# Accumulating DMAs in place of VectorE additions for the weight sums of a seven-product matrix multiplication

## The chip, the cores and the metric

The kernel runs on one core of a Trainium2 chip. A core has a matrix engine (TensorE, "PE" in the profile; its weight loads are "PEld"), a vector engine (VectorE, "DVE"), an activation engine (ScalarE, "ACT"), a general engine (GpSimd, "POOL") and a queue engine that mostly starts transfers (SyncE, "SP"). Each works through its own instructions in order and waits on semaphores for the others. Transfers (DMAs) are started from the queue of SP, ACT or POOL and carried out by 16 DMA engines. Data is worked on in SBUF (128 partitions); matrix products land in PSUM, which has eight banks here.

The metric is the device time of one execution in microseconds (us), as the median of several runs.

## The reference

Two sequences, 512 and 256 tokens of 1,024 features, go through two layers with shared weights. Each layer adds a SwiGLU feed-forward block, a token mixer and a second feed-forward block, all behind RMSNorms:

```
def swiglu_ffn(x, w1, w2):
    gate, up = jnp.split(x @ w1, 2, axis=-1)
    return (jax.nn.silu(gate) * up) @ w2

for li in range(DEPTH):                                   # DEPTH = 2
    x = x + 0.5 * swiglu_ffn(rmsnorm(x, norm_g[li, 0]), ffn_w1[li, 0], ffn_w2[li, 0])
    h = rmsnorm(x, norm_g[li, 1])
    x = x + mixer(h)           # a gated linear recurrence in layer 0, windowed attention in layer 1
    x = x + 0.5 * swiglu_ffn(rmsnorm(x, norm_g[li, 2]), ffn_w1[li, 1], ffn_w2[li, 1])
return rmsnorm(x, final_norm_g)
```

All is float32. `w1` is 1,024 x 5,632 (gate and up side by side), `w2` is 2,816 x 1,024. There are four feed-forward blocks, called f0 to f3 below.

## The kernel before

**Tiling of a feed-forward block.** The 768 tokens of both sequences are handled together, features on the partitions. The 2,816 hidden features are 22 blocks of 128, in groups of 2, 4, 4, 4, 4 and 4. For each group the kernel computes the hidden blocks ("up phase") and then multiplies them with their rows of `w2` and adds the result to x ("down phase"). Every operand is split into a high part (rounded to the matrix engine's float32r format) and a low part (the rest), and every product is three matmuls: high·high, high·low, low·high (`mm3`, lines 234 to 236).

**The seven-product pair.** The first group (2 blocks) uses plain products (`up_plain`). In the other five groups each hidden block is one pair of a gate tile and an up tile, each 1,024 x 128, multiplied with Strassen's scheme in Winograd's form (`up_pair`, from line 504): the two weight tiles are cut into halves a11, a12 (gate, first and last 512 rows) and a21, a22 (up), and the tokens into two halves of 384. Seven products of half size replace eight. They run on PE in the order p1, p6, p2, p7, p5, p4, p3, each as 12 matmuls of 384 columns (line 494). A pair has four PSUM banks, a, b, c and d, and between the products VectorE and ScalarE read them: for example `w = c - v` (line 516) reads bank c after p7 and must have read it before p4 accumulates into the same bank. The products need four sums of weight blocks: s3 = a11 + a21, a21 + a22, a11 + (a21 + a22), and a12 + that.

**Staging of weights.** `load_next` starts the loads of raw weights from SyncE into four buffers of 512 KB (`wr`), so two pairs at a time. `pair_steps` gives seven steps, one for each product. A step forms its sum on VectorE (lines 177, 178, 179 and 183) and calls `split` (lines 165 to 170): a ScalarE cast makes the high part (line 167), a VectorE subtraction the low part (line 168; on GpSimd for p5 alone). The result goes into one of eight buffers (`w`, `WBUFS`). When PE has finished a product, `done` frees its buffer and `ahead` stages the next step; so in the up phase the cast of a product waits until PE has finished the product eight places before it. Weights of the first group and of `w2` are split without sums (lines 152 and 153) and take two buffers each.

**Start of a block.** The token side needs sums too (t1 to t4 for each of four blocks, `sum_steps`, lines 411 to 414), formed on GpSimd while PE runs the first group's plain products; each is then split by ScalarE and VectorE (lines 239 and 240). After them, in ScalarE's order, come the activations of the plain products (line 485) and the split of their hidden block (line 239), which the first down phase waits for.

**Order.** A scheduler places the instructions of each engine when the program is built, from dependences and its own cost model; within an engine the order is then fixed. Buffers of one tag are used in turn; a new tile waits until the readers of the old one are done.

The functions that the change touches, with the line numbers that the profile of this kernel uses:

Of the kernel before, what the change touches and what calls it, by code (L numbers as in the profile page):

```python
# [9 lines left out]
F32 = mybir.dt.float32  # L10
# [3 lines left out]
ALU = mybir.AluOpType  # L14
AX = mybir.AxisListType

P = 128
# [4 lines left out]
TA, TB = 512, 256  # L22
# [20 lines left out]
class Trunk:  # L43
# [22 lines left out]
        return t[:, :n]  # L66

    def tmp(self, n, dt=F32):
        tag, bufs, size = ("tA", 9, TA) if n > TB else ("tB", 4, TB)
        t = self.tp.tile([P, size], dt, tag=tag, name=self.name(tag), bufs=bufs)  # L70
        return t[:, :n]

# [61 lines left out]
    def load_next(self):  # L134
        key, srcs, shape, eng = self.queue.pop(0)
        raws = []
        for src in srcs:
            t = self.wp.tile([P, 1024], F32, tag="wr", name=self.name("wr"), bufs=RAWBUFS)
            raw = t[:, : shape[0] * shape[1]].rearrange("p (a b) -> p a b", a=shape[0])
            self.last_load = self.nc.sync.dma_start(raw, src.rearrange("(k p) c -> p k c", p=P))  # L140
            raws.append(raw)
        steps = self.plain_steps(key, raws[0], shape, eng) if len(raws) == 1 else self.pair_steps(key, *raws)
        self.loaded.append((len(raws), steps))

    def wtile(self):
        return self.wp.tile([P, 1024], F32R, tag="w", name=self.name("w"), bufs=WBUFS)
# [8 lines left out]

        return [(2, go)]

    def pair_steps(self, key, one, two):
        nc = self.nc
        flat = lambda t, h: t[:, h * 4 : h * 4 + 4, :].rearrange("p a b -> p (a b)")  # L160
        a11, a12, a21, a22 = flat(one, 0), flat(one, 1), flat(two, 0), flat(two, 1)
        box = {}

        def split(name, src, eng):
            w = self.wtile()
            hi, lo = w[:, :512], w[:, 512:]
            nc.scalar.copy(hi, src)  # L167
            eng.tensor_sub(lo, src, hi.bitcast(F32))  # L168
            view = lambda t: t.rearrange("p (a b) -> p a b", a=4)
            self.staged[(*key, name)] = (view(hi), view(lo), 1)  # L170

        def p1():
            split("p1", a11, nc.vector)

        def p6():
            box["s3"] = self.tmp(512)
            nc.vector.tensor_add(box["s3"], a11, a21)  # L177
            nc.vector.tensor_add(a21, a21, a22)
            nc.vector.tensor_add(a11, a11, a21)
            split("p6", a11, nc.vector)  # L180

        def p3():
            nc.vector.tensor_add(a12, a12, a11)
            split("p3", a12, nc.vector)

        return [
            (1, p1),
            (1, p6),
            (1, lambda: split("p2", a12, nc.vector)),
            (1, lambda: split("p7", box["s3"], nc.vector)),  # L190
            (1, lambda: split("p5", a21, nc.gpsimd)),
            (1, lambda: split("p4", a22, nc.vector)),
            (1, p3),
        ]

    def stage_next(self):
# [223 lines left out]
    h = [None, None]  # L420
# [939 lines left out]
```

## Time and profile before

| | |
|---|---|
| median of 3 runs | 3043.2 us (3041.46 to 3043.63) |
| the profiled execution: time, span | 3045.14 us, 3043.3 us |
| mean granted TensorE clock | 0.978 |
| PE busy / PEld busy | 2935.9 us (96%) / 2722.8 us (89%) |
| DVE busy | 2013.2 us (66%), 3510 instructions |
| ACT busy | 1175.8 us (39%) |
| POOL busy | 570.2 us (19%), 414 instructions |
| moved by DMAs | 207.61 MB, 68 GB/s over the span |

Busy shares are averages over stages with different limits. A row of the groups of instructions names line, engine, operation, output and inputs with shape, and the count; after the first bar stand busy time in us and the mean of one in ns; after the second bar the idle time of the engine just before them and what ended it. In the timeline the columns are start, duration, engine, line, operation, operands, count, and in brackets the idle time before with its releaser. Names carry no buffer number: `wr` is a raw weight buffer, `w` a staged one, `ps` a PSUM bank, `big` an activation tile.

### The profile page before, as it was taken

To read this page: it belongs to the slowest core of one execution; us is meant where nothing else is said; L and a number is where in the kernel's file an instruction comes from. 1 tells how busy PE (TensorE), PEld (TensorE's weight loads), DVE (VectorE), ACT (ScalarE), POOL (GpSimd) and SP (SyncE) were. 2 spreads that over 40 slices of the span, in tenths; PEclk is the share of its full clock that TensorE was granted. 3 is DMA by queue.
4 is the path that set the end of the run, shared out by engine and by line. 5 is a ranking of instruction groups with operands and counts; after the bars stand their busy time and mean duration, and the time that the engine had idled before them with its cause. 6 is when DMAs were issued, how large, how long until landed. Compare 5 with 4: busy or idle time off the path is not lost. (4 is left out here: it accounts for less than half of the span.)

```text
span 3043.3 us, 42529 instructions
## 1 busy us (share of the span) xinstructions
PE 2935.9 (96%) x16805; PEld 2722.8 (89%) x16805; DVE 2013.2 (66%) x3510; ACT 1175.8 (39%) x2233; POOL 570.2 (19%) x414
## 2 busy tenths in 40 slices
PE   6999999999999999999999899999999998999998
PEld 6999999788898888999998899999887777999998
DVE  5766666467577667666666766666659867666665
ACT  5333334433333333333324333333457743333323
POOL 3000000344444123000002300000202433000001
PEclk8999999999999999999999899999999998999999
DMA  3212223321111231222123122212411111222122
GB/s 119 73 56 70 70 70 92 97 62 36 40 51 29 82 99 42 63 77 83 57 66 100 30 76 78 72 54 70 131 63 56 42 42 42 63 76 83 56 67 94
DMA packets 292041, 207.61 MB, mean 68 GB/s; under 512 B 7208, under 2 KB 275968, under 8 KB 291840
## 3 DMA queue, kind: packets, MB, share of 16 engines
q1 hardware_dynamic: 281920, 191.45, 21.1%
q10 hardware_dynamic: 9920, 13.43, 1.3%
q8 instruction: 132, 2.16, 0.3%
q14 instruction: 69, 0.57, 0.1%
HBM read 195.42 MB, written 9.44 MB: 67 GB/s over the span
## 5 line engine op out<-in xcount | busy, mean ns | idle before, releaser
L494 PE MATMUL ps<-big,w 128*128 128x384 f32 x6720 | 1171.1, 334 | 0.0
L494 PEld LDWEIGHTS ps<-big,w 128*128 128x128 f32 x6720 | 1163.4, 188 | 3.7 <-DVE tA L518 3.7
L234 PE MATMUL ps<-big,w 128*128 128x256 f32 (+2 forms) x2304 | 793.8, 347 | 30.9 <-ACT big L239 30.9
L235 PE MATMUL ps<-big,w 128*128 128x256 f32 (+2 forms) x2304 | 789.4, 343 | 6.8 <-DVE big L240 4.1
L236 PE MATMUL ps<-big,w 128*128 128x256 f32 (+2 forms) x2304 | 784.6, 341 | 0.0
L167 ACT CAST w<-wr 128x512 fp32r<-128x512 f32 x480 | 290.1, 621 | 834.1 <-issue 330.4
L234 PEld LDWEIGHTS ps<-big,w 128*128 128x128 f32 x2304 | 444.7, 193 | 78.9 <-ACT big L239 35.3
L235 PEld LDWEIGHTS ps<-big,w 128*128 128x128 f32 x2304 | 445.8, 193 | 51.5 <-DVE big L240 6.5
L236 PEld LDWEIGHTS ps<-big,w 128*128 128x128 f32 x2304 | 444.7, 193 | 42.0
L168 POOL TENSOR_TENSOR w<-wr,w 128x512 fp32r<-128x512 f32 x80 | 102.9, 1286 | 1656.2 <-ACT w L167 1656.2
L542 DVE SCALAR_TENSOR_TENSOR x<-ps,x 128x512 f32<-128x512 f32 (+1 forms) x384 | 210.7, 556 | 251.9 <-PE ps L236 250.8
L168 DVE TENSOR_TENSOR w<-wr,w 128x512 fp32r<-128x512 f32 x400 | 284.7, 725 | 69.7 <-ACT w L167 61.6
L152 ACT CAST w<-wr 128x1024 fp32r<-128x1024 f32 x192 | 201.3, 1050 | 227.9 <-PE ps L235 96.0
L153 DVE TENSOR_TENSOR w<-wr,w 128x1024 fp32r<-128x1024 f32 x124 | 151.4, 1223 | 74.4 <-PE ps L494 65.4
L153 POOL TENSOR_TENSOR w<-wr,w 128x1024 fp32r<-128x1024 f32 x68 | 167.2, 2468 | 177.0 <-ACT w L152 175.7
L240 DVE TENSOR_TENSOR big<-tA,big 128x384 fp32r<-128x384 f32 x240 | 160.7, 685 | 22.3 <-ACT big L239 22.1
L239 ACT CAST big<-tA 128x384 fp32r<-128x384 f32 x240 | 121.2, 513 | 104.8 <-DVE tA L521 33.5
L235 PE MATMUL ps<-w,big 128*128 128x512 f32 x336 | 134.3, 400 | 6.4 <-DVE w L153 6.4
L234 PE MATMUL ps<-w,big 128*128 128x512 f32 x336 | 137.6, 410 | 0.0
L735 DVE TENSOR_TENSOR big<-big,big 128x384 f32<-128x384 f32 x168 | 124.4, 787 | 18.5 <-ACT big L713 16.8
L236 PE MATMUL ps<-w,big 128*128 128x512 f32 x336 | 134.0, 399 | 0.0
L518 DVE TENSOR_TENSOR tA<-tA,ps 128x384 f32<-128x384 f32 x80 | 44.2, 553 | 91.4 <-PE ps L494 91.4
(194 smaller groups left out, 2964.3 us busy)
## 6 DMA issues: line engine op xcount, KB each, us to landing
wr<-in_ffn_w_dram SPq DMA_DIRECT2D x280, 512.0 KB, 3.9
wr<-in_hg_w_in_dram SPq DMA_DIRECT2D x40, 512.0 KB, 3.9
wr<-in_hg_w_o_dram SPq DMA_DIRECT2D x12, 512.0 KB, 4.0
wr<-in_sw_w_qkv_dram SPq DMA_DIRECT2D x12, 512.0 KB, 3.9
spill<-x ACTq DMA_DIRECT2D x16, 256.0 KB, 3.1
x<-spill ACTq DMA_DIRECT2D x16, 256.0 KB, 2.7
wr<-in_sw_w_o_dram SPq DMA_DIRECT2D x8, 512.0 KB, 3.5
out_dram<-tA SPq DMA_DIRECT2D x12, 256.0 KB, 2.0
```

The costliest lines, as they stand in the source:

```text
L152: self.nc.scalar.copy(hi, raw)
L153: eng.tensor_sub(lo, raw, hi.bitcast(F32))
L167: nc.scalar.copy(hi, src)
L168: eng.tensor_sub(lo, src, hi.bitcast(F32))
L234: nc.tensor.matmul(out, a[0], b[0], start=first, stop=False)
L235: nc.tensor.matmul(out, a[0], b[1], start=False, stop=False)
L236: nc.tensor.matmul(out, a[1], b[0], start=False, stop=last)
L239: self.nc.scalar.copy(hi, src)
L240: self.nc.vector.tensor_sub(lo, src, hi.bitcast(F32))
L494: self.nc.tensor.matmul(ps, a[x], b[y], start=first and k == 0 and i == 0, stop=k == 3 and i == 2, skip_group_check=True,)
L542: self.nc.vector.scalar_tensor_tensor(x, ps, c, x, ALU.mult, ALU.add)
L735: eng.tensor_mul(xv, xv, t[td][1 - par])
```

## The change

The four sums of each pair leave VectorE. Each becomes a DMA from SBUF to SBUF that adds its source to its destination, started from GpSimd's queue (`into`). The sums into the raw tiles are in place, as before. s3 gets a buffer of its own, one for all pairs: an extra load from HBM brings the first half of the up tile (256 KB) there, and a DMA adds a11. The s3 and a21 sums are issued right after the loads, the a11 sum after p1's split, the a12 sum after p2's split. Temporary buffers of the large kind go from nine to eight. The number of products, casts and low-part subtractions stays as it is.

In the program that is built, GpSimd's order for pairs in the middle of a group is: s3 of pair i, a11 of pair i, a21 of pair i+1, a12 of pair i, the low part of p5 of pair i, then s3 of pair i+1. From line 141 on, lines carry numbers 4 to 11 higher in the new file.

```diff
-        tag, bufs, size = ("tA", 9, TA) if n > TB else ("tB", 4, TB)
+        tag, bufs, size = ("tA", 8, TA) if n > TB else ("tB", 4, TB)
...
             raws.append(raw)
+        if len(raws) == 2:
+            s3 = self.wp.tile([P, 512], F32, tag="s3", name=self.name("s3"), bufs=1)
+            three = srcs[1].rearrange("(k p) c -> p k c", p=P)[:, :4, :]
+            self.last_load = self.nc.sync.dma_start(s3.rearrange("p (a b) -> p a b", a=4), three)
+            self.into(s3, raws[0][:, :4, :].rearrange("p a b -> p (a b)"))
+            one, two = (raws[1][:, h : h + 4, :].rearrange("p a b -> p (a b)") for h in (0, 4))
+            self.into(one, two)
+            raws.append(s3)
...
+    def into(self, out, src):
+        self.nc.gpsimd.dma_start(out, src, accum_op=ALU.add)
...
         def p1():
             split("p1", a11, nc.vector)
-
-        def p6():
-            box["s3"] = self.tmp(512)
-            nc.vector.tensor_add(box["s3"], a11, a21)
-            nc.vector.tensor_add(a21, a21, a22)
-            nc.vector.tensor_add(a11, a11, a21)
-            split("p6", a11, nc.vector)
-
-        def p3():
-            nc.vector.tensor_add(a12, a12, a11)
-            split("p3", a12, nc.vector)
+            self.into(a11, a21)
+
+        def p2():
+            split("p2", a12, nc.vector)
+            self.into(a12, a11)
 
         return [
             (1, p1),
-            (1, p6),
-            (1, lambda: split("p2", a12, nc.vector)),
-            (1, lambda: split("p7", box["s3"], nc.vector)),
+            (1, lambda: split("p6", a11, nc.vector)),
+            (1, p2),
+            (1, lambda: split("p7", s3, nc.vector)),
             (1, lambda: split("p5", a21, nc.gpsimd)),
             (1, lambda: split("p4", a22, nc.vector)),
-            (1, p3),
+            (1, lambda: split("p3", a12, nc.vector)),
         ]
```

More of the change, by code (lines that the diff above doesn't have):

```diff
@@ L141, in load_next @@
             raws.append(raw)
+        if len(raws) == 2:
[6 more added lines that the diff above has]
+            raws.append(s3)
         steps = self.plain_steps(key, raws[0], shape, eng) if len(raws) == 1 else self.pair_steps(key, *raws)
-        self.loaded.append((len(raws), steps))
+        self.loaded.append((len(srcs), steps))
+    def into(self, out, src):
+        self.nc.gpsimd.dma_start(out, src, accum_op=ALU.add)
     def wtile(self):
@@ L156, in plain_steps, with pair_steps @@
         return [(2, go)]
-    def pair_steps(self, key, one, two):
+    def pair_steps(self, key, one, two, s3):
         nc = self.nc
@@ L161, in pair_steps @@
         a11, a12, a21, a22 = flat(one, 0), flat(one, 1), flat(two, 0), flat(two, 1)
-        box = {}
         def split(name, src, eng):
```

## The prediction

> **What bounds the kernel now.** First the page's span and busy times, with the costliest group; then the table by stage of one group of f3 (up, then down); then the chain of waits there.
>
> ```profile
> span 3043.3 us, 42529 instructions
> PE 2935.9 (96%) x16805; PEld 2722.8 (89%) x16805; DVE 2013.2 (66%) x3510; ACT 1175.8 (39%) x2233; POOL 570.2 (19%) x414
> ...
> L494 PE MATMUL ps<-big,w 128*128 128x384 f32 x6720 | 1171.1, 334 | 0.0
> ```
> ```profile
> 2568.00:2627.00 59.00, 59.00 (x342) 58.77 (x341) 41.29 (x69) 25.44 (x44) 3.88 (x3) 1.00 0.30 89
> 2627.00:2660.00 33.00, 33.00 (x192) 29.05 (x190) 17.91 (x29) 4.56 (x8) 1.29 (x1) 1.00 0.11 33
> ```
> ```profile
> 2568.37 58.41 PE ps L494 x336
> ...
> 2660.28 58.38 PE ps L494 x336
> ```
>
> The columns of the stage table after the length are PE, PEld, DVE, ACT, POOL, clock, DMA share, GB/s. In the up phase PE is busy in all 59.00 us at clock 1.00, VectorE in 41.29. Line 494 has no idle before it, and the chain runs through its 336 matmuls without a break: 58.41 / 4 = 14.60 us for a pair, 2.09 for a product. So a faster VectorE gains nothing in the pairs; what can change there is only for the worse. PE's idle time that VectorE or ScalarE ends lies at the starts of the blocks (below).
>
> **What is removed.** The four additions of each pair, in the groups by line:
>
> ```profile
> L179 DVE TENSOR_TENSOR wr<-wr,wr 128x512 f32<-128x512 f32 x80 | 55.3, 692 | 2.8
> L183 DVE TENSOR_TENSOR wr<-wr 128x512 f32<-128x512 f32 x80 | 55.3, 691 | 2.1
> L178 DVE TENSOR_TENSOR wr<-wr 128x512 f32<-128x512 f32 x80 | 54.8, 685 | 0.1
> L177 DVE TENSOR_TENSOR tA<-wr,wr 128x512 f32<-128x512 f32 x80 | 54.7, 684 | 17.0 <-DMA wr<-in_ffn_w_dram 16.9
> ```
>
> 55.3 + 55.3 + 54.8 + 54.7 = 220 us of VectorE, all beside a saturated PE: worth 0, except at the starts.
>
> **What is added.** Per pair four DMAs from GpSimd of 256 KB each and one 256 KB load: 320 DMAs and 80 loads. The trace has no DMA from GpSimd and none that adds. Call L the time from "its semaphores are there" to "the sum has landed". The nearest rows are the issues, with median us to landing:
>
> ```profile
> wr<-in_ffn_w_dram SPq DMA_DIRECT2D x280, 512.0 KB, 3.9
> spill<-x ACTq DMA_DIRECT2D x16, 256.0 KB, 3.1
> x<-spill ACTq DMA_DIRECT2D x16, 256.0 KB, 2.7
> ...
> out_dram<-tA SPq DMA_DIRECT2D x12, 256.0 KB, 2.0
> ```
>
> Lower end: the fastest 256 KB row, 2.0. Upper end: twice the 512 KB row, 7.8. An adding DMA reads two operands of 256 KB, which is nearest to the 512 KB row, 3.9; for GpSimd's own work to issue it I add 1.1 (between 0 and the 1.29 us of its 128x512 subtraction, below). I take L = 5.0, an estimate. The extra load I put at 3.1 (256 KB row). In the up phase the DMA share is 0.30, so the engines themselves have room; contention is part of the width of L.
>
> The Trainium skill, page "DMA: Bandwidth & Descriptors", section "Anatomy of one DMA — SWDGE (gpsimd) path", fits a DMA from GpSimd as 2.0 us plus bytes over 436 GB/s; an estimate by it is 2.6 us for 256 KB, nothing being said of adding, and the sum would then be that of the second rival.
>
> **Where L is on the path.** The casts of the next pair's weights stand in ScalarE's and VectorE's order between the reads of the present pair's PSUM banks, on which PE waits. One pair of f3, whose products begin at 2660.28:
>
> ```profile
> 2662.40 0.48 ACT L510 COPY tA<-ps 128x384 f32<-128x384 f32 x1 [1.02 <-PE ps L494]
> 2663.01 0.62 ACT L167 CAST w<-wr 128x512 fp32r<-128x512 f32 x1
> 2664.54 0.62 ACT L167 CAST w<-wr 128x512 fp32r<-128x512 f32 x1 [0.91 <-PE ps L494]
> 2666.62 0.62 ACT L167 CAST w<-tA 128x512 fp32r<-128x512 f32 x1 [1.46 <-PE ps L494]
> ```
> ```profile
> 2667.27 0.69 DVE L168 TENSOR_TENSOR w<-tA,w 128x512 fp32r<-128x512 f32 x1 [0.66 <-ACT w L167]
> 2668.64 0.56 DVE L516 TENSOR_TENSOR tA<-ps,tA 128x384 f32<-128x384 f32 x1 [0.68 <-PE ps L494]
> ```
> ```profile
> 2669.39 1.29 POOL L168 TENSOR_TENSOR w<-wr,w 128x512 fp32r<-128x512 f32 x1 [15.52 <-ACT w L167]
> ```
>
> Let T be the end of p1 on PE (here 2662.37). Then come the casts of the next pair's p6 (2663.01), p2 and p7, p7's low part, done at 2667.96 = T + 5.6, and only then L516, which PE needs before p4, at T + 8.3 (four products after p1). In the new program's order p6, p2 and p7 still stand ahead of L516. Now p6's cast waits for the a11 sum to land, at X: from X, three casts (some 1.8) and the last low part (0.6) make p7 done at D = X + 2.4, and L516 with its waits is done at X + 3.1. So PE stalls by X + 3.1 − (T + 8.3).
>
> X hangs on the pair before: the one s3 buffer is free at D of that pair, then load 3.1, s3 sum L, and the a11 sum L, which must wait because s3's DMA reads a11. So X(next) = D + 3.1 + 2L, and the loop takes 2.4 + 3.1 + 2L = 5.5 + 2L against PE's 14.6. It breaks even at L = 4.55. Before, this loop was additions of 0.69 us.
>
> For one group, from the start of its up phase: T(1) = 2.1, T(2) = 16.7, T(3) = 31.3, later by stalls. The second pair's s3 has been formed in the down phase before, so X(2) = 2.0 + L (after p1's split; two splits come at once there). With L = 5: X(2) = 7.0, no stall (10.1 against 10.4); D(2) = 9.4; X(3) = 22.5, stall 25.6 − 25.0 = 0.6; D(3) = 24.9; X(4) = 38.0, stall 41.1 − 40.2 = 0.9. The fourth pair stages w2 tiles, which have no sums. 1.6 us a group, 5 groups in 4 blocks: 20 x 1.6 = **32 us**. The same steps give 0 at L = 4.5, 82 at 5.5, 152 at 6.2 and 312 at 7.8.
>
> The DMA issues on GpSimd are 4 x 1.1 = 4.4 us of 14.6, and p5's subtraction behind them has seven products of lead. SyncE waits longer before its loads, but a raw tile is loaded a pair ahead.
>
> **The starts of the blocks.** Rows of f1, f2 and f3: p1's low part, the last hidden split, PE's wait.
>
> ```profile
> 1175.61 0.68 DVE L168 TENSOR_TENSOR w<-wr,w 128x512 fp32r<-128x512 f32 x1
> 1713.38 0.69 DVE L168 TENSOR_TENSOR w<-wr,w 128x512 fp32r<-128x512 f32 x1
> 2544.53 0.69 DVE L168 TENSOR_TENSOR w<-wr,w 128x512 fp32r<-128x512 f32 x1
> 2547.76 0.69 DVE L177 TENSOR_TENSOR tA<-wr,wr 128x512 f32<-128x512 f32 x1 [1.81 <-DMA wr<-in_ffn_w_dram]
> ```
> ```profile
> 1181.03 0.51 ACT L239 CAST big<-tA 128x384 fp32r<-128x384 f32 x1 [2.32 <-DVE tA L486]
> 1721.16 0.51 ACT L239 CAST big<-tA 128x384 fp32r<-128x384 f32 x1 [3.61 <-DVE tA L486]
> 2550.28 0.51 ACT L239 CAST big<-tA 128x384 fp32r<-128x384 f32 x1 [2.65 <-DVE tA L486]
> ```
> ```profile
> PE ps L234 <- ACT big L239: 30.9, 7, 8.2
> ...
> 1181.59 1.01 PE L234 MATMUL ps<-big,w 128*128 128x512 f32 x2 [3.74 <-ACT big L239]
> 1721.73 0.96 PE L234 MATMUL ps<-big,w 128*128 128x512 f32 x3 [1.77 <-ACT big L239]
> 2550.84 1.01 PE L234 MATMUL ps<-big,w 128*128 128x512 f32 x2 [3.51 <-ACT big L239]
> ```
>
> L486 stood behind the additions, even behind a second pair's L177 that waited for its load; that goes. But in the new order the last hidden split stands behind p6, p2 and p7, so behind one L: it ends 2.3 after p1's low part plus L. p1's low part I take as done at 1175.3 (before at 1176.3; an addition ahead of it is gone), 1714.1 (as before) and 2544.7 (before 2545.2, additions ahead of it gone). Against the ends 1181.54, 1721.67 and 2550.79 that is L − 3.9, L − 5.3 and L − 3.8: with L = 5, +1.1 − 0.3 + 1.2 = **+2 us**. In f0 GpSimd must issue two DMAs amid the sums of the tokens, and wait for a load; I take +1 (less than one issue, since its later sums wait for others). The eighth temporary I put at 0: one of the nine held s3.
>
> **Sum.** 32 + 2 + 1 = 35. The profiled execution took 3045.1 (its span 3043.3 and 1.8 around it), so 3080 against it; the median of the runs is 1.9 lower: **3078 us**, 1.1% slower.
>
> **The rivals.**
> 1. *Heavier chain*, L over 6.2: the same loop, e.g. because the adding DMAs and loads collide or GpSimd issues slowly. Over 152 + 6 + 1 us: 3202 and more, to 3366 at L = 7.8 (312 + 10 + 1). For it: none of these DMAs is in the trace; against it: the share 0.30. Chance 0.12.
> 2. *Hidden*, L from 2.7 (the reload row) to 4.6: seven products of lead and a loop under 14.6 cover all; the starts give −3 (−1.2, −1.8 as f2's gap has no more, −1.1, f0 +1) to +2: 3040 to 3045, no change. For it: at L = 2.7 the loop is 10.9, 3.7 under PE's pace; against it: the second operand and GpSimd's issue would have to cost next to nothing. Chance 0.26. The Trainium skill's page named above speaks for this rival; no run here shows its figure.
> 3. *Faster*: the waits 3.74, 1.77 and 3.51 at the starts close, since nothing on VectorE blocks L486 any more. It decides from L under about 2.3, and gives at L = 2.0 −1.9, −1.8 and −1.8, and up to 0.7 each for an addition that stood ahead of an earlier split: about 3036. Against it: L at the fastest row. Chance 0.06.
>
> **How the numbers follow.** The forecast (L 4.6 to 6.2; 3046 to 3202) has 0.56, the rivals 0.12, 0.26 and 0.06. A change of 0.2% (6 us) is about what can be told. The range takes in the hidden case, 2 us wider for the spread of the runs, and leaves out the heavier and the faster: 3038 to 3202. Slower 0.56 + 0.12, less 0.02 for its lower edge: 0.66; within 0.2%: 0.28; faster 0.06.
>
> **What would show it.** The groups by line lose the four VectorE additions; the DMA issues gain 320 rows from POOL with their time to landing (L, right if 4.6 to 6.2). PE's L498 (the old 494) shows idle before it, ended by VectorE's L520 (the old 516), some 20 to 40 waits of 0.5 to 2 us in the third and fourth pairs of the groups; ScalarE's L177 casts are released by DMAs. The forecast is wrong if L498 has no idle (hidden), or if stalls stand in every pair and at the down phases too (heavier).

## The result, and the profile after

The changed kernel takes 3068.1 us (median; 3064.8 to 3076.3) beside 3042.3 us (3034.9 to 3043.6) for the kernel before on the same chip: a ratio of **1.0094, 95% interval 1.0068 to 1.0120**. The forecast was 3078 (3038 to 3202), slower with a chance of 0.66. The profiled execution took 3067.5 us with a span of 3065.6, against 3045.1 and 3043.3 before.

In the new file PE's line 494 is 498, the casts and low parts of the pairs are lines 177 and 178 (167 and 168 before), the accumulating DMA is line 154, the load of s3 line 145, and the bank read `w = c - v` is line 520 (516). From the page of the changed kernel, the span, the busy times and the groups that answer to those shown before:

```profile
span 3065.6 us, 43632 instructions
PE 2937.1 (96%) x16805; PEld 2712.0 (88%) x16805; DVE 1829.3 (60%) x3190; ACT 1158.0 (38%) x2233; POOL 850.8 (28%) x734
...
L498 PE MATMUL ps<-big,w 128*128 128x384 f32 x6720 | 1181.8, 335 | 14.1 <-DVE tA L520 10.6
L177 ACT CAST w<-wr 128x512 fp32r<-128x512 f32 x480 | 286.4, 618 | 974.6 <-DMA wr<-wr 511.5
```

Line 498 is the reading that matters. Busy and idle together are the time of all 20 up phases: 1181.8 + 14.1 = 1195.9 us, against 1171.1 + 0.0 before, so **+24.8 us in the up phases**. Of the 14.1 idle, 10.6 are ended by line 520. ScalarE's casts now wait 511.5 us for DMAs into `wr`, and VectorE, 184 us lighter, gains the kernel nothing. PE's waits by releaser:

```profile
PE ps L498 <- DVE tA L520: 10.6, 18, 1.6
```

The columns are the sum, the number and the longest; 3 more waits (3.2 us) are ended by ScalarE's line 514. The 18 of line 520 begin in two places of a group: 8 (3.3 us) at 25.1 to 26.5 us after its start, 10 (7.3 us) at 39.7 to 41.7, that is before p4 of the second and of the third pair; line 520 ends none at the down phases. The DMA issues with their median time from issue to landing:

```profile
wr<-wr POOLq DMA_DIRECT2D x240, 256.0 KB, 3.9
s<-in_ffn_w_dram SPq DMA_DIRECT2D x80, 256.0 KB, 3.4
s<-wr POOLq DMA_DIRECT2D x80, 256.0 KB, 4.0
```

One median hides four kinds of sum. Taken issue by issue, a12's sum, with the load of s3 started some 0.3 us behind it, lands after 4.9 us (median of 79; 4.2 to 7.4), s3's after 4.0 (3.2 to 6.2), and a21's, issued when a load has just landed, after 3.3 (median of 50).

The +22.3 us of the span fall as follows, by the first and last product of each up phase: up phases +24.9, down phases +2.0, the start of f0 +3.6 (its first product at 100.4 us, not 96.8), the end +0.7, and the three stretches between the blocks −8.9. This last is not the change's work: the control of experiment 2, which differs from the change in one temporary, has 1193.2 us there, as the kernel before. The windowed-attention mixer before f3 with the same matmuls, first before, then after (columns as in the prediction's stage table):

```profile
2187.00:2544.00 357.00, 328.75 (x1804) 281.92 (x1804) 269.15 (x705) 220.73 (x567) 125.58 (x112) 0.94 0.17 51
```
```profile
2206.60:2556.60 350.00, 321.94 (x1805) 277.04 (x1805) 266.87 (x703) 220.80 (x567) 127.71 (x114) 0.96 0.18 52
```

PE is busy 6.8 us less for one matmul more, at a granted clock of 0.96 against 0.94. So single profiles differ by some 10 us outside the pairs, and the experiments are read first by line 498, which has clock 1.00 in all up phases of both kernels.

### One group, step by step

Second group of f3 after the change, whose products begin at 2676.42 (groups are counted here among the five that use pairs); X is the start of the casts that wait for the a11 sum.

```profile
2683.15 1.14 ACT L177 CAST w<-wr 128x512 fp32r<-128x512 f32 x2 [3.97 <-DMA wr<-wr]
...
2685.02 0.68 DVE L178 TENSOR_TENSOR w<-s,w 128x512 fp32r<-128x512 f32 x1
...
2685.39 0.86 POOL L154 DMA_DIRECT2D wr<-wr  x1 [2.14 <-DVE w L178]
...
2685.73 0.37 SPq L145 DMA_DIRECT2D s<-in_ffn_w_dram  x1
...
2689.64 0.88 POOL L154 DMA_DIRECT2D s<-wr  x1 [2.06 <-DMA s<-in_ffn_w_dram]
2690.42 0.62 ACT L177 CAST w<-wr 128x512 fp32r<-128x512 f32 x1 [2.72 <-DMA wr<-wr]
...
2692.26 0.52 ACT L243 CAST big<-tA 128x384 fp32r<-128x384 f32 x1 [1.23 <-DVE tA L525]
2692.68 0.62 ACT L177 CAST w<-wr 128x512 fp32r<-128x512 f32 x1
...
2693.33 0.69 DVE L178 TENSOR_TENSOR w<-wr,w 128x512 fp32r<-128x512 f32 x1
...
2695.70 0.86 POOL L154 DMA_DIRECT2D wr<-wr  x1 [5.18 <-DVE big L244]
...
2699.11 1.14 ACT L177 CAST w<-wr 128x512 fp32r<-128x512 f32 x2 [4.07 <-DMA wr<-wr]
...
2701.58 0.55 DVE L520 TENSOR_TENSOR tA<-ps,tA 128x384 f32<-128x384 f32 x1
...
2702.18 0.44 PE L498 MATMUL ps<-big,w 128*128 128x384 f32 x1 [0.64 <-DVE tA L520]
```

The last two rows are the stall: line 520 stands in VectorE's order behind the low parts that wait for X, and PE waits 0.64 us for it. Two chains run from X = 2683.15 to the next X = 2699.11.

*Loop S*, the prediction's: p7's low part ends at D = 2685.70; the one s3 buffer is free, its load is issued at 2685.73; s3's DMA follows at 2689.64, lands 5.4 us later at 2695.04 (its own row below), and lets the a11 DMA start at 2695.70 (VectorE's L244, which the row names, has nothing to do with a11). That lands after 3.3 us and X follows. D to D: 3.94 + 5.4 + 0.66 + 3.41 + 2.56 = 15.97 us against PE's 14.6. This s3 sum is the third slowest of the 40 that lie in such turns (two in each of the 20 groups); by the medians of the 40 the loop is 4.0 + 4.3 + 0.7 + 3.3 + 2.6 = 14.9 us.

```profile
s<-wr POOLq DMA_DIRECT2D x1, 256.0 KB, 5.4
```

*Loop A*, not in the prediction: p2's low part lets the a12 DMA go at 2685.39; it lands some 5 us later and p3's cast starts at 2690.42. Behind this cast, in ScalarE's order, stand a token cast (2692.26) and then p1's cast of the next pair (2692.68). Its low part ends at 2694.02; only then may the a11 sum go. Here that is 1.7 us before S lets it start; in the first group of f3 the two are within a few tenths. Over the 40 turns neither loop is the one that binds: 21 of the a11 sums are issued 0.54 us after the end of p1's low part (A came last), 14 within 0.65 us of s3's landing (S came last), 4 when both had just ended and 1 by neither. Both loops hold two landings, and both are a little over 14.6; A alone would have taken 10.87 to the end of p1's low part + 0.54 + 3.41 = 14.8 in this turn.

Loop A also stops PE directly. Line 514, a bank read that p2 needs, stands in ScalarE's order behind p3's cast. In the first group of f3 the a12 sum lands after 6.9 us:

```profile
2628.00 0.62 ACT L177 CAST w<-wr 128x512 fp32r<-128x512 f32 x1 [5.41 <-DMA wr<-wr]
...
2632.15 0.45 PE L498 MATMUL ps<-big,w 128*128 128x384 f32 x1 [1.72 <-ACT tA L514]
```

All three waits that line 514 ends follow such a cast.

### The profile page after: what moved, and what is told of

It reads as the page before. It is cut to its first block, busy times and chain, and to the rows that moved or that the text cites. A ratio compares the mean times of both kernels' runs of the same rounds, so it can differ in the third digit from the quotient of the medians.

```text
span 3065.6 us, 43632 instructions
## 1 busy us (share of the span) xinstructions
PE 2937.1 (96%) x16805; PEld 2712.0 (88%) x16805; DVE 1829.3 (60%) x3190; ACT 1158.0 (38%) x2233; POOL 850.8 (28%) x734
## 3 DMA queue, kind: packets, MB, share of 16 engines
q0 software_dynamic: 46080, 83.91, 15.7%
## 5 line engine op out<-in xcount | busy, mean ns | idle before, releaser
L498 PE MATMUL ps<-big,w 128*128 128x384 f32 x6720 | 1181.8, 335 | 14.1 <-DVE tA L520 10.6
L177 ACT CAST w<-wr 128x512 fp32r<-128x512 f32 x480 | 286.4, 618 | 974.6 <-DMA wr<-wr 511.5
L178 DVE TENSOR_TENSOR w<-wr,w 128x512 fp32r<-128x512 f32 x400 | 302.7, 774 | 338.9 <-ACT w L177 337.6
L154 POOL DMA_DIRECT2D wr<-wr x240 | 206.9, 863 | 1013.9 <-DVE w L178 598.6
L244 DVE TENSOR_TENSOR big<-tA,big 128x384 fp32r<-128x384 f32 x240 | 163.6, 697 | 58.5 <-ACT big L243 51.5
L154 POOL DMA_DIRECT2D s<-wr x80 | 70.0, 875 | 368.1 <-DMA wr<-in_ffn_w_dram 188.9
L239 PE MATMUL ps<-w,big 128*128 128x512 f32 x336 | 133.2, 397 | 7.6 <-DVE w L164 7.6
L178 POOL TENSOR_TENSOR w<-wr,w 128x512 fp32r<-128x512 f32 x80 | 122.8, 1535 | 50.8 <-ACT w L177 48.4
L238 PE MATMUL ps<-w,big 128*128 128x512 f32 x336 | 136.6, 406 | 0.0
```

Source lines behind the costliest of these rows:

```text
L154: self.nc.gpsimd.dma_start(out, src, accum_op=ALU.add)
L238: nc.tensor.matmul(out, a[0], b[0], start=first, stop=False)
L239: nc.tensor.matmul(out, a[0], b[1], start=False, stop=False)
L244: self.nc.vector.tensor_sub(lo, src, hi.bitcast(F32))
L498: self.nc.tensor.matmul(ps, a[x], b[y], start=first and k == 0 and i == 0, stop=k == 3 and i == 2, skip_group_check=True,)
```

## The experiments

All ratios are against the kernel before, run on the same chip.

**1. Eight temporaries alone.** The kernel before with `("tA", 8, TA)` in place of `("tA", 9, TA)`.

> The kernel before with eight instead of nine of the large temporaries, nothing else. The prediction put this at 0: 3040 to 3045 us beside 3042. In the trace of the changed kernel the parts outside the feed-forward pairs are together some 9 us shorter; if that comes from the eighth temporary alone, this kernel takes about 3033 us.

3043.8 us, ratio 1.0003 [0.9993, 1.0014]; line 494 stays at 1171.4 us with no idle. The temporary costs nothing that can be told, and it does not shorten the mixers. In its trace f0's first product stands at 99.3 us, so 2.5 of the 3.6 us at f0 are seen without any of the DMAs.

**2. Two s3 buffers, and its control.**

```
-            s3 = self.wp.tile([P, 512], F32, tag="s3", name=self.name("s3"), bufs=1)
+            s3 = self.wp.tile([P, 512], F32, tag="s3", name=self.name("s3"), bufs=2)
-        tag, bufs, size = ("tA", 8, TA) if n > TB else ("tB", 4, TB)
+        tag, bufs, size = ("tA", 7, TA) if n > TB else ("tB", 4, TB)
```

> The changed kernel with two s3 buffers instead of one (and seven large temporaries, to make room). Theory S, the prediction's loop (PE stalls because the one s3 buffer comes free late, then load, s3 sum and a11 sum in a row): the loop is opened, PE's idle before L498 falls from 14.1 us to under 3 and the time from 3068 to about 3050. Theory A (the loop runs through the a12 sum, p3's cast and the next pair's p1, which stands behind that cast in ScalarE's order): idle stays at 10 to 17 us, time 3063 to 3073.

> The changed kernel with seven instead of eight large temporaries, nothing else: the control for the kernels with two s3 buffers. Without effect: 3063 to 3073. If the temporaries are what cost 10 us in the kernel with two s3 buffers (3078), this one takes 3075 to 3081.

3078.4 us, ratio 1.0118 [1.0099, 1.0137]; the control, with the second edit alone, 3072.7 us, 1.0094 [1.0080, 1.0108], as the changed kernel itself. Line 498 with two buffers:

```profile
L498 PE MATMUL ps<-big,w 128*128 128x384 f32 x6720 | 1184.0, 336 | 16.4 <-DVE tA L520 13.2
```

Up phases 1200.4 us: opening loop S gained nothing. The stalls at 40 us fell from 10 (7.3 us) to 5 (4.0), those at 25 us rose from 8 (3.3) to 11 (8.8). Two things took S's place. Loop A is there as before. And S had kept the DMAs apart: a11's had to wait until s3's had landed. With two buffers the s3 sum of a later pair is free to go, and in the first group of f3 it is issued 1.4 us ahead of a11's; the two, with a load from HBM beside them as well, land after 5.2 and 4.9 us:

```profile
2615.30 0.88 POOL L154 DMA_DIRECT2D s<-wr  x1 [5.65 <-DVE tA L528]
2616.71 0.86 POOL L154 DMA_DIRECT2D wr<-wr  x1 [0.53 <-DVE tA L530]
```

**3. The a12 sum back on VectorE.** Loop A is opened.

```
         def p2():
             split("p2", a12, nc.vector)
-            self.into(a12, a11)
+        def p3():
+            nc.vector.tensor_add(a12, a12, a11)
+            split("p3", a12, nc.vector)
```

> The changed kernel with the a12 sum back on VectorE just before p3's split; the three other sums stay accumulating DMAs. Theory A (a12 loop): p3's cast waits for no DMA, PE's idle before L498 falls to under 3 us, time about 3045 to 3050. Theory S (s3 loop): idle stays at 10 to 17 us, time 3063 to 3073.

3104.6 us, ratio 1.0201 [1.0184, 1.0218]: 36 us worse than the change. `w = c - v` is line 523 here:

```profile
L501 PE MATMUL ps<-big,w 128*128 128x384 f32 x6720 | 1188.9, 336 | 36.8 <-DVE tA L523 36.4
```
```profile
2621.20 0.37 SPq L145 DMA_DIRECT2D s<-in_ffn_w_dram  x1
...
2624.67 0.88 POOL L154 DMA_DIRECT2D s<-wr  x1 [2.34 <-DVE tA L527]
...
2629.78 0.86 POOL L154 DMA_DIRECT2D wr<-wr  x1 [4.24 <-DVE big L247]
...
2633.85 1.14 ACT L177 CAST w<-wr 128x512 fp32r<-128x512 f32 x2 [4.69 <-DMA wr<-wr]
...
2635.83 0.69 DVE L190 TENSOR_TENSOR wr<-wr 128x512 f32<-128x512 f32 x1
2636.44 0.68 DVE L178 TENSOR_TENSOR w<-s,w 128x512 fp32r<-128x512 f32 x1
```

This is loop S alone, D to D: 3.5 for the load, 5.1 until a11's DMA may start, 4.1 to X, 3.3 to D = 2637.12, then the next load: 15.95 us; the median of the 40 turns is 15.8, against 15.25 in the change. The addition (line 190) stands between X and D (3.3 instead of 2.6): it lengthens S and holds back line 523 by as much in every pair, so that PE has 31 waits where it had 18. Both theories missed the size; A as the only loop falls, since with it open S still stops PE.

**4. The s3 sum on VectorE**, the extra load kept.

```
-            self.into(s3, raws[0][:, :4, :].rearrange("p a b -> p (a b)"))
         def p1():
             split("p1", a11, nc.vector)
+            nc.vector.tensor_add(s3, s3, a11)
             self.into(a11, a21)
```

> The changed kernel with the s3 sum on VectorE behind p1's split (the extra load into the one s3 buffer stays); the three other sums stay accumulating DMAs. Theory S: its loop is shorter by one landing of 4 to 5 us, idle before L498 under 3 us, time 3045 to 3050. Theory A: the a12 loop is as it was, idle 10 to 17 us, 3063 to 3073.

3110.3 us, ratio 1.0221 [1.0204, 1.0237], line 498 at 1189.8 + 48.5. It does not tell the theories apart, since the edit made a stall of its own: VectorE's order now holds a wait for a load, ahead of a bank read (line 522, which ends 47.9 of the 48.5).

```profile
L183 DVE TENSOR_TENSOR s<-s,wr 128x512 f32<-128x512 f32 x80 | 55.4, 692 | 146.9 <-DMA s<-in_ffn_w_dram 136.2 <-DMA wr<-in_ffn_w_dram 10.6
```

**5. Both loops open**: the edits of 2 and 3 together.

> The changed kernel with two s3 buffers (seven large temporaries) and the a12 sum back on VectorE: the two edits of which each alone made it slower (3078 and 3105 us). Theory T (two loops of nearly the same length, each with two landings of some 5 us: S through the one s3 buffer, A through the a12 sum and ScalarE's order; opening one leaves the other): both are open now, PE's idle before the up products falls from 16 and 36 us to under 8 and the time to 3045 to 3055. Rival V (a sum on VectorE is itself what stalls, since it stands ahead of the PSUM reads there): idle stays over 25 us, 3090 to 3105.

3075.4 us, ratio 1.0099 [1.0083, 1.0115].

```profile
L501 PE MATMUL ps<-big,w 128*128 128x384 f32 x6720 | 1179.4, 335 | 13.5 <-DVE tA L523 13.3
```

Up phases 1192.9 us: better than either edit alone (1200.4 and 1225.7), but no real gain on the change, and the 3045 to 3055 expected were missed. What builds up from pair to pair is gone: 1 stall at 40 us (0.5 us) instead of 10. At 25 us there are still 11 (10.7 us), and 3 (2.1 us) at 10.6. In the first group of f3:

```profile
2606.80 0.69 DVE L178 TENSOR_TENSOR w<-wr,w 128x512 fp32r<-128x512 f32 x1
...
2607.66 0.88 POOL L154 DMA_DIRECT2D s<-wr  x1 [5.67 <-DVE w L178]
...
2608.25 1.18 POOL L154 DMA_DIRECT2D wr<-wr  x1
...
2613.79 1.14 ACT L177 CAST w<-wr 128x512 fp32r<-128x512 f32 x2 [4.96 <-DMA wr<-wr]
```

p1's low part ends at 2607.49; a11's DMA stands in GpSimd's order behind the s3 sum of a later pair, runs beside it, and X comes 6.3 us after the low part. PE waits 1.37 us. In the next pair no s3 sum is near, the a11 sum lands 3.3 us after its issue, X comes after 3.9 us and PE does not wait. So with both loops open, what is left is one landing on a chain with no room for it, made longer by its neighbour. All 20 groups agree: at this place the a11 sum is issued 0.6 to 1.1 us behind an s3 sum and lands after 3.8 to 5.6 us (median 4.3); in the next pair it has no sum near, lands after 3.3 in the median, and PE waits once in 20. The end of a load from HBM runs beside both.

**6. p3 on GpSimd, with two s3 buffers**: another way to open loop A, with nothing added on VectorE.

```
-            (1, lambda: split("p3", a12, nc.vector)),
+            (1, lambda: split("p3", a12, nc.gpsimd, nc.gpsimd.tensor_copy)),
```

> The changed kernel with two s3 buffers (seven large temporaries, loop S open) and p3's cast and low part both on GpSimd, so that the cast which waits for the a12 sum no longer stands ahead of p1's cast in ScalarE's order (loop A open), with no sum on VectorE. Theory T: neither loop is left, only the single chain p1's low part, a11 sum, casts, L520, which stalls at landings over some 5.2 us: PE's idle before L498 under 5 us, time 3045 to 3052. If one of the loops is not what it was taken for, or the mere presence of the accumulating DMAs slows the pairs, idle stays at 13 to 17 us, 3068 to 3080.

3137.5 us, ratio 1.0309 [1.0295, 1.0323]; line 498 at 1199.8 + 53.7. The expected 3045 to 3052 were far off, as loop A had not been opened but moved into GpSimd's order:

```profile
2740.17 1.15 ACT L177 CAST w<-wr 128x512 fp32r<-128x512 f32 x2 [4.57 <-DMA wr<-wr]
...
2742.41 0.86 POOL L154 DMA_DIRECT2D wr<-wr  x1 [2.01 <-DVE w L178]
...
2747.42 1.00 POOL L177 CAST w<-wr 128x512 fp32r<-128x512 f32 x1 [2.82 <-DMA wr<-wr]
...
2751.37 1.19 POOL L154 DMA_DIRECT2D wr<-wr  x1
...
2757.18 1.14 ACT L177 CAST w<-wr 128x512 fp32r<-128x512 f32 x2 [5.57 <-DMA wr<-wr]
```

From X: a12's DMA, 5.0 us to its landing, p3's cast and low part on GpSimd, and behind them, in the same queue, s3's DMA and a11's, which lands after 5.8: 17.0 us a pair. On GpSimd, too, the wait for one landing stands ahead of the issue of the next.

**7. The a11 sum back on VectorE.** It is the one landing that both loops and the chain left in 5 have in common.

```
         def p1():
             split("p1", a11, nc.vector)
-            self.into(a11, a21)
+        def p6():
+            nc.vector.tensor_add(a11, a11, a21)
+            split("p6", a11, nc.vector)
```

> The changed kernel with the a11 sum back on VectorE ahead of p6's split; s3, a21 and a12 stay accumulating DMAs, one s3 buffer, eight temporaries. Theory T: loop S is D + 3.4 + 4.8 + 0.7 + 3.3 = some 12 us, loop A is 2.3 + 5.1 + 3.6 + 0.7 = some 12 us, both under PE's 14.6: idle before L498 under 3 us, time 3040 to 3048. Rival V (sums on VectorE stall the PSUM reads): as slow as the two other kernels with one sum on VectorE, 3095 to 3110.

**3036.1 us, ratio 0.9975 [0.9963, 0.9986]**: faster than both kernels, and than expected.

```profile
L501 PE MATMUL ps<-big,w 128*128 128x384 f32 x6720 | 1171.5, 334 | 0.0
```
```profile
PE ps L241 <- ACT big L246: 22.3, 7, 6.9
```

240 accumulating DMAs and 80 loads are still there, a12's and s3's landings are as long as before (4.8 and 5.8 us in the second group of f3), and PE waits for none of them. The rival that a VectorE sum is itself the stall falls. The second row is the gain: PE's waits at the starts of the blocks, 30.9 us before the change, are 22.3. The three that the prediction listed (3.74, 1.77 and 3.51) are down to 1.00, 0.28 and 1.00, 6.7 us less; the waits just ahead of them are 1.8 us less in all.

**8. a11 and a12 on VectorE**, only s3 and a21 by DMA.

> a11 and a12 sums on VectorE as before the change; s3 and a21 (formed when the pair is loaded) stay accumulating DMAs with the extra load. Theory T: nothing in a pair waits for a landing that is not some 10 us old, idle before L498 under 2 us; at the starts of the blocks VectorE no longer waits for loads ahead of its other work, 0 to -5 us: 3037 to 3045 us. Rival V: 3090 and more.

3037.4 us, ratio 0.9979 [0.9969, 0.9989], as expected; up phases 1171.7 us, the same 22.3 us at the starts. The intervals of 7 and 8 overlap.

**9. The same DMAs without adding.**

```
-        self.nc.gpsimd.dma_start(out, src, accum_op=ALU.add)
+        self.nc.gpsimd.dma_start(out, src)
```

> The changed kernel with its four DMAs as plain copies: same issue, sources and destinations, nothing is added (so the four sums are left out of what is computed). If the second operand is what makes a landing long (3.9 us median after the issue, against 2.0 to 3.1 of the 256 KB rows of before), it falls to 2.5 to 3.2 us, both loops go under 14.6 us and the time to 3040 to 3050 us. If the time is that of the path (GpSimd's issue, the queue), it stays at 3.6 to 4.0 us and 3060 to 3070 us.

3046.8 us, ratio 1.0009 [1.0000, 1.0018], and no wait in the up phases:

```profile
L498 PE MATMUL ps<-big,w 128*128 128x384 f32 x6720 | 1171.7, 335 | 0.0
...
L154 POOL DMA_DIRECT2D wr<-wr x240 | 129.1, 538 | 1063.6 <-DVE w L178 584.8
...
wr<-wr POOLq DMA_DIRECT2D x240, 256.0 KB, 2.5
...
s<-wr POOLq DMA_DIRECT2D x80, 256.0 KB, 4.3
```

As expected of the first case: same queues, dependences and bytes, and the whole loss in the pairs comes from the extra time of the sums, in issue and landing. GpSimd issues a copy in 0.54 us instead of 0.86, and a copy into `wr` lands after 2.5 us instead of 3.9. (s3's lands after 4.3 here too, so the second operand is not what lengthens that one.) It shows as well that taking the four sums off VectorE is worth nothing in the pairs.

**10. Each sum as two DMAs of 128 KB.**

```
+        for h in (slice(0, 256), slice(256, 512)):
+            self.nc.gpsimd.dma_start(out[:, h], src[:, h], accum_op=ALU.add)
```

> The changed kernel with each sum as two accumulating DMAs of 128 KB (256 columns each), issued one behind the other. If what counts is the bytes, each half lands some 2.9 us after its issue, the sum is there about as early as before and the time stays at 3060 to 3075. If most of the landing time is a fixed cost of a DMA, the halves land 3.6 us and more after their issues, the sum is later by most of one more issue (0.86 us), so about 5.6 us after its semaphores: by the prediction's loop over 80 us of stalls, 3110 to 3150.

3104.1 us, ratio 1.0203 [1.0189, 1.0217].

```profile
L499 PE MATMUL ps<-big,w 128*128 128x384 f32 x6720 | 1190.2, 336 | 36.9 <-DVE tA L521 30.3
...
wr<-wr POOLq DMA_DIRECT2D x480, 128.0 KB, 3.4
```

Half the bytes land after 3.4 us instead of 3.9, and the second half is issued 0.9 us later. Up phases 1227.1 us, +56 on the kernel before. The direction is that of a mostly fixed cost; the size, 3104, is just under the 3110 to 3150 expected of it. With 9 this makes a scale: more landing time, more stall, and none at 2.5 us.

**11. s3 and a21 as additions on GpSimd**, in the kernel before, with no DMA.

```
-            nc.vector.tensor_add(box["s3"], a11, a21)
-            nc.vector.tensor_add(a21, a21, a22)
+            nc.gpsimd.tensor_add(box["s3"], a11, a21)
+            nc.gpsimd.tensor_add(a21, a21, a22)
```

> The kernel before with the s3 and a21 sums as additions on GpSimd instead of VectorE, no DMA and no extra load. If the 9 us that the kernels with a11 (or a11 and a12) on VectorE save at the starts of the blocks come from VectorE having no sum ahead of the block's own work that waits for a load, this kernel saves them too: waits at the starts 3.7, 1.8 and 3.5 us gone, 3034 to 3040. If VectorE's a11 sum now waits for GpSimd there instead (two additions of some 1.3 us behind the loads), the waits stay: 3042 to 3055.

3057.8 us, ratio 1.0048 [1.0035, 1.0061]. Neither of the two. At the starts of f1 and f3 the waits of 3.74 and 3.51 us shrank to 1.06 each and in f2 the 1.77 to 0.33, though the waits ahead of them in f1 and f2 grew by 1.6 and 1.5 (in f3 that wait fell by 1.3): in part the expected gain. But the down phases grew from 533.2 to 549.5 us in sum:

```profile
2633.31 1.29 POOL L178 TENSOR_TENSOR wr<-wr 128x512 f32<-128x512 f32 x1
2633.37 1.65 DVE L521 TENSOR_TENSOR tA<-tA,tA 128x384 f32<-128x384 f32 x1
...
2639.50 0.61 PE L234 MATMUL ps<-big,w 128*128 128x512 f32 x2 [0.90 <-ACT big L239]
```

In this group, the first of f3, GpSimd adds while VectorE works on the group's last hidden tiles: line 521, with a mean of 0.55 us before, takes 1.65, the steps behind it come later, and PE waits 0.9 us at the start of the down phase. There are 16 such waits in the down phases, 12 us in all.

## Why the prediction was right, and where it was not

- **"A faster VectorE gains nothing in the pairs; what can change there is only for the worse."** Right: with the sums gone and the landings short (9), line 498 is 1171.7 us as before.
- **L = 5.0.** Right for a12's sum, 5.3 us from p2's low part to p3's cast (median), which the prediction had on no path. Too large for the loop that it was meant for: S's two landings are 9.5 us, 4.75 each, in the turn shown, but by the medians of the 40 turns 4.3 for s3's, 0.7 to the issue of a11's and 3.3 to X, 8.3 in all, 4.2 each. That is under the break-even of 4.55. S comes to 14.6 and over only because its load took 4.0 us from D to the issue of the s3 sum, where the prediction put 3.1, and because some s3 sums are slow (up to 6.2). Wrong as a reading rule too: the text said that L is right if the landing rows show 4.6 to 6.2, and they show 3.9 and 4.0. A median over four kinds of sum, counted from the issue, is not the time from "semaphores there" to "landed" of the sum that is waited for; by those rows alone the hidden rival would have been the better reading.
- **The Trainium skill's 2.6 us.** The Trainium skill, page "DMA: Bandwidth & Descriptors", section "Anatomy of one DMA — SWDGE (gpsimd) path", gives 2.6 us for 256 KB as an estimate by its fit. The plain copies of 9 into `wr` agree with it (2.5), and the time then, 3046.8 us, is close to the 3040 to 3045 of the hidden rival; for an adding DMA the measurement decides, 3.3 with no load beside it and 3.9 to 4.9 in the medians of the change.
- **The stall, "1.6 us a group", 32 us.** The two stalls of 0.6 and 0.9 add up to 1.5, so 30. Measured 24.8 in the up phases, 1.2 a group, mostly in the two places that the steps gave (stalls at 25.0 and 40.2 us; seen from 25.1 and 39.7 on, while the third and the fourth pair are staged and PE works on the second and third), with 21 waits where 20 to 40 of 0.5 to 2 us were named; only 9 of them reach 0.5. What PE waits for, and where, was right: a landing ahead of the casts, and line 520 behind them. The path to it was right in part: the prediction's loop S held back 14 of the 40 a11 sums and loop A 21, and the 3.2 us at line 514 come from a12 alone. So the nearness of 32 to 24.8 is in part luck: L was too large for S, the load too small, and a second loop of about the same length was left out. Of these 24.8 us only 14.1 are idle time before a matmul; the other 10.7 stand in the same line's busy time. Some 8 of them go with the stalls (an estimate): matmuls start every 0.174 us and last 0.334, so each of 27 stalls hides 0.16 us in that overlap, and the eight matmuls after it lose another 0.13.
- **What the prediction left out: the a12 sum.** It counted as one of four DMAs to issue and was never put on a path, though p3's cast, which waits for it, stands in ScalarE's order ahead of the next pair's p1. That is loop A, about as long as S. What S alone would have cost, no run shows without another edit in it; but a remedy taken from the prediction, a second s3 buffer, gains nothing (2), and taking a12 away alone loses (3).
- **"p5's subtraction ... seven products of lead", the issues on GpSimd.** Right, no stall is ended by them.
- **The starts.** "+1.1 − 0.3 + 1.2 = +2": the waits went from 3.74, 1.77 and 3.51 to 4.03, 3.69 and 4.02, so +0.3, +1.9 and +0.5, +2.7 in all; that sum was near, the shares not, and the waits just ahead of them, which the prediction left as they were, fell by 1.8. f0: +1 taken, +3.6 seen, of which 2.5 also stand in a kernel without the DMAs (1).
- **The sum.** 32 + 2 + 1 was 24.8 + 2.7 + 3.6 and 2.0 in the down phases (0.1 us each, not foreseen): 33 against 35. The profiled span grew by 22.3 only, because the three stretches between the blocks, with these 2.7 in them, came out 8.9 shorter: PE was busy 11.2 us less there, at granted clocks of 0.982, 0.894 and 0.953 against 0.975, 0.908 and 0.933. The medians differ by 25.8.
- **The rivals.** *Hidden* is what experiment 9 looks like; 10 goes towards *heavier* (3104 us) and stays short of its 3202. *Faster* had its waits right, those at the starts, which shrink by 6.7 us in 7 against the 5.5 to 7.6 worked out. Its condition, L under 2.3, was not necessary. It needs only the a11 sum kept off the DMAs (7), and the prediction did not look at the four sums one by one.

Two things could make a12's sum land after 4.9 us: the load of s3 (0.3 us behind it) and GpSimd's subtraction (0.6 us). The nine kernels with accumulating DMAs of 256 KB (the change and experiments 2 to 8, with the control) tell them apart. Take the sums with no other sum issued within 3.2 us of them, and look at their first 3.2 us. With no load from HBM in flight they land after 3.3 us in the median, with GpSimd's own work beside them (112 sums) as without (324). With a load in flight for 2 us or more it is 4.93 with that work (230) and 4.75 without (650). So it is the load that makes the landing long.

What stays open: why the nearness of another sum lengthens a landing in experiment 5 (0.6 to 1.1 us apart, 4.3 us) and not in the group shown above, where the a11 and a21 sums are issued 1.5 us apart and both land after 3.3; and what S alone costs.

## What to carry to other kernels

Price each moved operation by its own place in the chain: a transfer whose result is due in 10 us is free at 5 us of landing, and the same transfer between two casts of one pair is not. Count landings per round trip, not DMAs: loops with two of them were a little over PE's 14.6 us a pair, loops with one left no wait (7), and opening one of two loops of about equal length gained nothing, so look for the link that all of them share. And ask of every wait which engine's order it stands in, for all that is queued behind it waits too, be it on ScalarE, VectorE or GpSimd.

## What the runs showed of the hardware

- An accumulating DMA of 256 KB within SBUF lands 3.3 us after its issue when no load and no other sum is near (436 sums of nine kernels; also the median of the 50 sums of a21 in the change), a copy of the same size after 2.3 (median of 45 in experiment 9); GpSimd's issue takes 0.86 us against 0.54. For the same 83.91 MB the packets of the sums take 15.7% of the 16 engines' time over the span, those of the copies 7.9%. Beside loads from HBM the median is 4.8 to 4.9 us, and single sums take up to 7.6, with the DMA engines at a share of 0.61 in the up phases of f3 (0.30 before), so room on average says little of one landing.
- Small two-input operations of VectorE and GpSimd's subtractions and additions slow each other where they run at the same time: 1.65 us instead of 0.55 for line 521 (11), and in the changed kernel a VectorE low part of 1.39 instead of 0.69 beside a GpSimd one of 1.61 instead of 1.28. The rows of the changed kernel, second group of f3:

```profile
2701.92 1.61 POOL L178 TENSOR_TENSOR w<-wr,w 128x512 fp32r<-128x512 f32 x1
2702.70 1.39 DVE L178 TENSOR_TENSOR w<-wr,w 128x512 fp32r<-128x512 f32 x1
```

The Trainium skill, page "SBUF — State Buffer", section "Who interferes with whom", states that a VectorE instruction with two inputs in SBUF contends with a GpSimd instruction that reads SBUF; these rows agree.
